# Hybrid encoder layer on one core: the 32 sample tokens taken out of the second half's tiles, computed as one chain for all four heads

## The chip, the cores and the metric

The kernel runs on one core of a Trainium2 chip. The core has a matmul engine (PE, with its weight loads shown apart as PEld), a vector engine (DVE), an activation engine (ACT), a general engine (POOL) and a queue that issues most transfers (SP). Each engine works through its own list of instructions in order and waits on semaphores where it needs what another engine made. The metric is the device time of one execution in microseconds (us); lower is better.

## The reference

One encoder layer is applied to 2048 prompt tokens and, with the same weights, to 32 sample tokens that continue a running stream. What is computed for each of the two groups:

```python
h = rmsnorm(x, g_pre_mix)
z = h @ w_in                                  # 1024 x 2560
u, zq, zf, zi, zg = split(z, [512, 1024, 1536, 2048])
u_ext = concat([pool_hist, u])                # 15 rows of history ahead
y_pool = pool_mix(u_ext, ...)                 # window means over 2/4/8/16 frames minus the frame, per group a linear map
q = silu(zq); fgate = lb + (1 - lb) * sigmoid(zf)
kin = (1 - lb) * sigmoid(-zf); logf = log(fgate)
S1, o = hgrn_run(S0, q, kin, zi, logf)        # gated recurrence, 4 heads x 128, evaluated in chunks
y_hg = rmsnorm(o, g_hg_norm) * silu(zg)
x = x + rmsnorm(concat([y_pool, y_hg]) @ w_out, g_post_mix)
x = x + rmsnorm((silu(h2 @ w_gate) * (h2 @ w_up)) @ w_down, g_post_ffn)   # h2 = rmsnorm(x, g_pre_ffn)
```

The outputs are y for both groups, the last 15 rows of u_ext and the final states S1 of both. The sample tokens start from a given history (15 x 512) and given states (4 x 128 x 128).

## The kernel before, in words

The prompt is worked in two halves of 1024 tokens. Each half goes through the same stages: the value columns of the input product (tile `vps`), for each of four heads the f, q and g columns and then the recurrence (`hgrn`), the four pooling groups, the output product (`project`, tile `ops`), the gate and up products (tiles `gx`, `gy`, `gz`, `gw`). At the end the down product runs over both halves (`dx`, `dy`, `dz`). Large products split each float32 operand into a high and a low part and take three fast 128x512 matmuls for one exact one (`hi`, `lo` in the tile names; `mmb` is the bank of the input product). Small products run on plain float32 operands; each such matmul leaves two records in the profile, a transpose leaves one.

In `hgrn` a head's 1024 tokens are handled in levels: `group` issues 32 small matmuls into the bank `gb`, then `merge` multiplies keys on POOL (`k_t`) and queries on DVE (`qa`) by the gate products of that level, and the next level's `group` needs both. Then come transposes of k (`kps`), state updates (`ups`), outputs (`ops2`, shown as `ops` in the trace), and transposes back (`yps`).

The 32 sample tokens ride with the second half. They are columns 1024 to 1055 of the tiles f, k, q, g and qa (slots of 1088 columns). For each of the 16 column tiles of the second half `sample_tile` multiplies the normalized sample tokens `hsr` with the raw weights in four column groups (`fps`, 8 matmuls), and a step later adds the four parts by a small matmul (`fst`, `fps`). `group` has a 33rd matmul for them, `merge` runs over 1056 columns, and each head ends with a block of its own (L1004 to L1021): one transpose `kps`, three matmuls `ups`, one transpose `yps`, with a state load and a state store. Pooling handles the sample columns in extra small windows (L1051, L1054).

What sets the order: PE's list is written out by the program. Generators (`Task`) hold side work; each `yield` names how much PE time must pass before the next step, and `poll` runs steps that are due after every third large matmul. So a small matmul stands a set number of large matmuls behind what it needs. `join` issues waiting `fps` blocks together with the next `group`. The lists of the other engines are ordered by a scheduler at build time.

Of the kernel before, what the change touches and what calls it, by code (L numbers as in the profile page):

```python
# [29 lines left out]
NT = 21  # L30
# [4 lines left out]
TMAX = HALF + NS  # L35
SLOT = HALF + 64
# [44 lines left out]
def body(tc, ins, outs, cst):  # L81
    nc = tc.nc
    ctx = ExitStack()
    with ctx:
# [69 lines left out]
        roots = DP.tile([1, TMAX], F32, name="roots")  # L154
# [270 lines left out]

        COL_Q, COL_F, COL_I, COL_G = 512, 1024, 1536, 2048
# [5 lines left out]
        def make_half(B):  # L432
            S = Half()
            S.B = B
            S.T = TMAX if B else HALF
# [19 lines left out]
        def later_stats(S):  # L455
# [10 lines left out]
            xs = t2("xsl", [NS, 512]), t2("xsl", [NS, 512])  # L466
            for c in range(2):
                nc.sync.dma_start(out=xs[c], in_=x_s[:, c * 512:c * 512 + 512])
                sumsq(xs[c], NS, st[0:NS, 32 + c:33 + c])
            del xs  # L470
# [7 lines left out]
            nc.gpsimd.tensor_tensor(rt[0:NS, 16:17], st[0:NS, 32:33], st[0:NS, 33:34], ALU.add)  # L478
            nc.gpsimd.tensor_scalar(rt[0:NS, 16:17], rt[0:NS, 16:17], 1.0 / D, EPS, ALU.mult, ALU.add)
            nc.gpsimd.tensor_tensor(rt[0:NS, 17:18], rt[0:NS, 16:17], nhalf[0:NS, 0:1], ALU.pow)  # L480
            roots_out(rt, NCH, roots[0, 0:HALF])
            nc.sync.dma_start(out=roots[0, HALF:TMAX].rearrange("(p i) -> p i", i=1), in_=rt[0:NS, 17:18])

# [19 lines left out]
        def front_norm(S, tg):  # L503
            if tg == 0:
                S.hsr = SP.tile([P, KD, NS], F32, tag="hs", name="hsr", bufs=1)
                S.ysr = SP.tile([P, KD, NS], F32, tag="ysr", name="ysr", bufs=1)
# [3 lines left out]
            if tg == 1:  # L510
                rq = t2("rbs", [P, NS])
                nc.sync.dma_start(out=rq, in_=roots[0:1, HALF:TMAX].broadcast_to([P, NS]))
                nc.sync.dma_start(out=S.hsr, in_=ins["x_sample_channels"].rearrange("(k p) t -> p k t", p=P))
# [3 lines left out]
            if tg == 1:  # L517
                nc.vector.tensor_tensor(S.hsr, S.hsr, rq.unsqueeze(1).broadcast_to([P, KD, NS]), ALU.mult)
                nc.vector.tensor_tensor(S.hsr, S.hsr, g_pre.unsqueeze(2).broadcast_to([P, KD, NS]), ALU.mult)
            yield from scaled_channels(S, tg)  # L520
# [21 lines left out]
        def first_values(S):  # L542
# [41 lines left out]
            nc.sync.dma_start(out=cons[:, 0:C_VEC], in_=cst[:, 0:C_VEC])  # L584
            xg = {}
# [113 lines left out]
            for k in range(0, KD, 2):  # L699
                scaled(k, 0)  # L700

        def values(S, tg):
# [4 lines left out]
            for k in range(0, KD, 2):  # L707
# [12 lines left out]
                if smp:  # L720
                    for kk in range(2):
                        four.add(S.hsr[:, k + kk, :], raw[:, kk * 512:kk * 512 + 512])
            for i in range(4):
                (nc.vector.tensor_copy if i % 2 else nc.scalar.copy)(S.vt[tg * 4 + i], pss[i])
            if smp:
                S.vs = t2("vs")
                nc.gpsimd.memset(S.vs, 0.0)
                sample_sum(S.vs[P - NS:P], sps, 4)

        def sample_tile(S, w, use):  # L730

            if not S.B:
                return None
            raw = w[0]

            def whole():
                task.begun = True
                ps = axbank("fps")
                for k in range(KD):
                    q = k % 4  # L740
                    mm(ps[32 * q:32 * q + 32, 0:P], S.hsr[:, k, :], raw[:, k * P:(k + 1) * P], k < 4, k >= 4, 60.0)
                st = t2("fst", [P, P])
                nc.vector.tensor_copy(st, ps[:, 0:P])
# [8 lines left out]
            return task  # L752
# [8 lines left out]
        def head_products(S, h):  # L761
            H = Half()
            H.f, H.k, H.q, H.g = (ztile(n) for n in ("f_t", "k_t", "q_t", "g_t"))
            def use_f(ps, n0=HALF, n1=TMAX):
# [8 lines left out]
            def use_q(ps, n0=HALF, n1=TMAX):  # L773
# [5 lines left out]
            def use_g(ps, n0=HALF, n1=TMAX):  # L779
# [11 lines left out]
            def tile_of(use):  # L791
                w = take()
                smp = sample_tile(S, w, use)
                blocks_of(w, use, S.blocks)
                return smp

            if h == 0 and not S.B:
                wf, wq = take(), take()
                for blk in S.blocks:
                    blocks_of(wf, use_f, [blk])  # L800
                    blocks_of(wq, use_q, [blk])
            else:
                H.smp = [tile_of(use_f), tile_of(use_q)]
            if h == 0:
                S.attn = [t2(f"attn{i}", [P, 4, P]) for i in range(2)]
                both = [t2(f"cmp{i}") for i in range(2)]
                S.cmp = [tl[:, 0:P].rearrange("p (c x) -> p c x", x=32) for tl in both]
                S.cmps = both[1][:, P:2 * P]
                for tl in S.attn + both:
                    nc.gpsimd.memset(tl, 0.0)  # L810
            task = Task(hgrn(S, H, h), (1800.0 if S.B else 3000.0), after=S.hgrn)
            tile_of(use_g)
# [7 lines left out]
        def hgrn(S, H, h):  # L820
            B, T = S.B, S.T
            for tk in H.smp if B else ():
                tk.finish()
            f_t, k_t, q_t, g_t, vt = H.f, H.k, H.q, H.g, S.vt
            attn, cmp_ = S.attn, S.cmp
            qa = ztile("qa")
            tt = ztile("tt")
            nc.vector.tensor_tensor(qa[:, 0:T], q_t[:, 0:T], f_t[:, 0:T], ALU.mult)
            gb = [axbank("gb") for _ in range(2)]
            blks = [(c, j) for c in range(NCH) for j in range(4)] + [(NCH, 1)] * B  # L830

            def place(c, j, a, b):
                if c < NCH:
                    return gb[c // 4][32 * j:32 * j + 32, c % 4 * 96 + a:c % 4 * 96 + b]
                return gb[1][32:64, 448 + a:448 + b] if b <= 64 else gb[0][32:64, 384 + a:384 + b]

            def group(goff, src, pick, n=16):
                join()
                for c, j in blks:
                    c0 = c * P + 32 * j if c < NCH else HALF  # L840
                    mm(place(c, j, goff, goff + n), k_t[:, c0:c0 + 32], pick(src[:, c0:c0 + 32]), True, True, 36.0)

            def half_of(L):
                return lambda ap: ap.rearrange("p (a two l) -> p a two l", two=2, l=L)[:, :, 1, :]

            toff = 0

            def merge(m, tcur):
                nonlocal toff
                L = 1 << m  # L850
                n = T if m < 5 else HALF
                na = n // (2 * L)
                qv = qa[:, 0:n].rearrange("p (a two l) -> p a two l", two=2, l=L)[:, :, 1, :]
                kv = k_t[:, 0:n].rearrange("p (a two l) -> p a two l", two=2, l=L)[:, :, 0, :]
                tv = tcur[:, 0:2 * na].rearrange("p (a two) -> p a two", two=2)
                nxt = tt[:, toff:toff + na]
                toff += na
# [5 lines left out]
            def masked(dst, view, row0, nch, r):  # L863
                for i in range(NGRP):
                    mk = cons[row0:row0 + r, C_MASK + 16 * i:C_MASK + 16 * i + 16].bitcast(I32).unsqueeze(1).broadcast_to([r, nch, 16])
                    src = view(16 * i, 16 * i + 16) if i in (0, 3, 4, 5) else view(16, 48)
                    if i == 1 or i == 2:
                        src = src.rearrange("p c (b y) -> p c b y", y=4)[:, :, :, 2 * i - 2:2 * i]
                        mk = mk.rearrange("p c (b y) -> p c b y", y=2)
                    if i == 0:  # L870
                        o = dst.rearrange("p c (a two) -> p c a two", two=2)[:, :, :, 0]
                    elif i == 1:
                        o = dst.rearrange("p c (b y two) -> p c b y two", y=2, two=2)[:, :, :, :, 1]
                    elif i == 2:
                        o = dst.rearrange("p c (b two y) -> p c b two y", two=2, y=2)[:, :, :, 1, :]
                    else:
                        L = 1 << (i - 1)
                        o = dst.rearrange("p c (a two l) -> p c a two l", two=2, l=L)[:, :, :, 1, :]
                        mk = mk.rearrange("p c (a l) -> p c a l", l=L)
                        src = src.rearrange("p c (a l) -> p c a l", l=L)  # L880
                    nc.vector.copy_predicated(o, mk, src)

            group(0, q_t, lambda ap: ap.rearrange("p (a two) -> p a two", two=2)[:, :, 0])
            yield 0.0
            tc_ = merge(0, f_t)
            fb = f_t[:, 0:T].rearrange("p (b y) -> p b y", y=4)
            for dst, src in ((fb[:, :, 0:2], q_t[:, 0:T].rearrange("p (b y two) -> p b y two", y=2, two=2)[:, :, :, 1]),
                             (fb[:, :, 2:4], half_of(2)(qa[:, 0:T]))):
                nc.scalar.copy(dst, src)
            yield 5000.0  # L890
            group(16, f_t, lambda ap: ap, 32)
            yield 0.0
            tc_ = merge(1, tc_)
            for m in (2, 3, 4):
                yield (STEP + 900.0 * (h + 1 == NH and m == 4)) if S.B else 1200.0 + 700.0 * (m == 3 and h + 1 < NH)
                group(16 * (m + 1), qa, half_of(1 << m))
                yield 0.0
                tc_ = merge(m, tc_)
# [927 lines left out]
```

## Time and profile before

| | |
|---|---|
| time, 3 runs | 2080.56, 2083.34 and 2084.01 us, median 2083.34 |
| span of the profiled execution | 2079.3 us (its time outside the span is not shown) |
| DMA moved | 319.49 MB, mean 154 GB/s |
| first half: values, columns with recurrence and pooling, output product, gate and up | from 5, 50, 284 and 374 us |
| second half: the same stages | from 797, 843, 1087 and 1184 us |
| down product of both halves | from 1636 us |

The page gives the busy time of each engine as a share of the span, the span in 40 slices, and the costliest groups of instructions. The span runs from the first to the last instruction of the core; the runs' times hold what lies around it too.

### The profile page before, as it was taken

Reading aid. Unit: us, or ns where it says so; the run is one execution under the profiler, and the core shown is the slowest. Engines: PE = TensorE matmul, PEld = TensorE weight load, DVE = VectorE, ACT = ScalarE, POOL = GpSimd, SP = SyncE. Lnnn points to the kernel's source line nnn. Section 1 sums busy time; section 2 is a strip of 40 time slices with the busy share of each in tenths; the row PEclk is TensorE's granted clock in tenths of the full one; section 3 lists DMA queues with packets and bytes.
Section 4 is the critical chain, followed back from the end, with each engine's and each line's share of the span. In section 5 each row is a group of like instructions: output and inputs, shape, how many; then the busy total and the mean of one; then the engine's idle time right before and its main releaser. Section 6 shows DMA issues by size and latency. Waiting matters only on the chain.

```text
span 2079.3 us, 34073 instructions
## 1 busy us (share of the span) xinstructions
PE 2068.0 (99%) x13093; PEld 1686.5 (81%) x13093; DVE 1418.5 (68%) x2288; ACT 834.6 (40%) x1656; POOL 279.7 (13%) x375
## 2 busy tenths in 40 slices
PE   9999999999999999999999999999999999999998
PEld 7788888888888888788888788888888778888876
DVE  5655665787777778465575697776666866566587
ACT  6444445654444445233334563444444521011032
POOL 0232302100000000122231200000000210110134
PEclk9999999999999999999999999999999999999999
DMA  8321144445555558211015614554445796776778
GB/s 288 115 88 42 44 142 162 132 127 167 161 153 152 157 172 260 70 46 36 26 54 177 200 52 137 163 149 139 147 137 173 231 335 203 218 226 200 219 223 220
DMA packets 391777, 319.49 MB, mean 154 GB/s; under 512 B 18216, under 2 KB 320800, under 8 KB 391616
## 3 DMA queue, kind: packets, MB, share of 16 engines
q1 hardware_dynamic: 389168, 309.41, 48.1%
q0 software_dynamic: 2016, 7.34, 1.9%
q8 instruction: 103, 1.69, 0.3%
q10 hardware_dynamic: 432, 0.57, 0.1%
q14 instruction: 58, 0.48, 0.1%
HBM read 216.79 MB, written 100.47 MB: 153 GB/s over the span
## 4 chain that ended last, share of the span: by engine, by line
PE 96%; DVE 2%; DMA 1%; ACT 0%; issue 0%; POOL 0%; DVEq 0%; SPq 0%; ACTq 0%; POOLq 0%
PE gx L202 23%; PE mmb L202 16%; PE gy L202 12%; PE dx L202 10%; PE ops L202 10%; PE gz L202 5%; PE dy L202 5%; PE vps L202 4%; PE dz L202 3%; PE gb L202 1%; PE gw L202 1%; PE gsps L202 1%; PE ups L202 1%; DVE acc L1605 1%; PE tps L345 1%; PE fps L202 1%
## 5 line engine op out<-in xcount | busy, mean ns | idle before, releaser
L202 PE MATMUL gx<-fhi,wf 128*128 128x512 f32 x1376 | 386.9, 391 | 0.0
L202 PEld LDWEIGHTS gx<-fhi,wf 128*128 128x128 f32 x1376 | 256.8, 188 | 54.9 <-issue 2.2
L202 PE MATMUL gx<-flo,wf 128*128 128x512 f32 x688 | 213.1, 390 | 0.0
L202 PE MATMUL gy<-fhi,wf 128*128 128x512 f32 x704 | 201.6, 390 | 0.0
L202 PE MATMUL dx<-dhi,hst 128*128 128x512 f32 x640 | 185.4, 391 | 0.8 <-DVE acc L1605 0.7
L202 PE MATMUL mmb<-hTlo,whi 128*128 128x512 f32 x512 | 175.3, 404 | 0.0
L202 PE MATMUL mmb<-hThi,whi 128*128 128x512 f32 x512 | 165.5, 404 | 0.0
L1605 DVE TENSOR_TENSOR acc<-dx,acc 128x512 f32<-128x512 f32 x168 | 115.1, 690 | 71.6 <-PE dx L202 70.6
L202 PE MATMUL mmb<-hThi,wlo 128*128 128x512 f32 x512 | 158.8, 391 | 0.0
L1325 DVE TENSOR_TENSOR wf<-s,wf 128x512 fp32r<-128x512 f32 x176 | 120.2, 690 | 56.0 <-ACT wf L1320 54.0
L202 PEld LDWEIGHTS gy<-fhi,wf 128*128 128x128 f32 x704 | 131.8, 188 | 28.1 <-DVE c L1427 0.4
L202 PEld LDWEIGHTS gx<-flo,wf 128*128 128x128 f32 x688 | 129.1, 188 | 27.0
L1320 ACT CAST wf<-s 128x512 fp32r<-128x512 f32 x176 | 108.1, 623 | 102.8 <-DVE s L1301 31.5
L202 PEld LDWEIGHTS dx<-dhi,hst 128*128 128x128 f32 x640 | 119.5, 188 | 30.1 <-issue 3.4
L1544 ACT CAST dhi<-t 128x1024 fp32r<-128x1024 f32 x20 | 20.7, 1055 | 249.8 <-DVE dlo L1545 181.6
L1325 DVE TENSOR_TENSOR wf<-wraw,wf 128x512 fp32r<-128x512 f32 x132 | 89.8, 687 | 34.4 <-ACT wf L1320 34.4
L202 PEld LDWEIGHTS mmb<-hTlo,whi 128*128 128x128 f32 x512 | 96.2, 188 | 20.5 <-issue 0.8
L202 PEld LDWEIGHTS mmb<-hThi,wlo 128*128 128x128 f32 x512 | 96.3, 188 | 18.9 <-issue 0.2
L1320 ACT CAST wf<-wraw 128x512 fp32r<-128x512 f32 x132 | 80.8, 622 | 75.8 <-PE gx L202 36.2
L202 PE MATMUL gy<-flo,wf 128*128 128x512 f32 x352 | 108.7, 389 | 0.0
L202 PEld LDWEIGHTS mmb<-hThi,whi 128*128 128x128 f32 x512 | 91.8, 188 | 20.6 <-issue 3.3
L202 PE MATMUL dx<-dlo,hst 128*128 128x512 f32 x320 | 98.6, 389 | 0.0
(326 smaller groups left out, 3974.8 us busy)
## 6 DMA issues: line engine op xcount, KB each, us to landing
hst<-hdFalse SPq DMA_DIRECT2D x140, 256.0 KB, 2.9
hst<-hdTrue SPq DMA_DIRECT2D x140, 256.0 KB, 3.0
wraw<-in_w_gate_dram SPq DMA_DIRECT2D x50, 512.0 KB, 4.0
wraw<-in_w_up_dram SPq DMA_DIRECT2D x50, 512.0 KB, 3.9
hdFalse<-hhi SPq DMA_DIRECT2D x77, 256.0 KB, 2.3
hdFalse<-hlo SPq DMA_DIRECT2D x77, 256.0 KB, 2.2
hdTrue<-hhi SPq DMA_DIRECT2D x77, 256.0 KB, 2.2
hdTrue<-hlo SPq DMA_DIRECT2D x77, 256.0 KB, 2.5
```

What stands on the lines that cost most here:

```text
L202: nc.tensor.matmul(out, l, r, start=start, stop=stop, skip_group_check=more)
L345: nc.tensor.transpose(ps[:, c:c + P], xn[:, (2 * kp + kk) * P:(2 * kp + kk + 1) * P], ident)
L1320: nc.scalar.copy(wf[:, 0], getattr(M, src) if isinstance(src, str) else src)
L1325: nc.vector.tensor_tensor(wf[:, 1], getattr(M, src) if isinstance(src, str) else src, wf[:, 0].bitcast(F32), ALU.subtract)
L1544: nc.scalar.copy(hi, src)
L1605: nc.vector.tensor_tensor(dst, ps, dst, ALU.add)
```

## The change

The sample tokens leave the tiles of the second half. Their raw channels are loaded at the start (`sample_loads`) and multiplied by g_pre on POOL; the tokens are loaded once more, four times over in the partitions, for their root mean squares (`sample_stats`). `sample_tile` now runs in the first half, when the same weight tiles pass, and scales by the root when it copies `fps` out; the results of all heads and groups lie in one tile `z` (128 channels x f, q, g, u x 4 heads x 32 tokens). After the values of the second half one task, `sample_mix`, does for all four heads at once what was done per head: gates, five levels on a 128-column tile (4 matmuls a level, bank `xgb`), one transpose `kps`, one output of five matmuls with a block matrix (`ops2`), one 512-wide state update (`ups`), one transpose back. The pooling windows of the prompt lose the 15 history columns ahead and run the first 31 columns in small tiles of their own (`eh`). The slots of the large pool shrink from 1088 to 1024 columns, and the pool of 512-column tiles has 25 buffers where it had 21.

```diff
-NT = 21
+NT = 25
...
-TMAX = HALF + NS
-SLOT = HALF + 64
+SLOT = HALF
...
+        def sample_loads():
+            Smp.hsr = SP.tile([P, KD, NS], F32, tag="hs", name="hsr", bufs=1)
+            Smp.z = SP.tile([P, 4, P], F32, tag="xz", name="xz", bufs=1)
...
+            nc.sync.dma_start(out=Smp.hsr, in_=ins["x_sample_channels"].rearrange("(k p) t -> p k t", p=P))
+            Smp.x = [t2("xs4") for _ in range(2)]
+            for q in range(8):
+                r, c = q // 2 * 32, q % 2
+                nc.sync.dma_start(out=Smp.x[c][r:r + 32], in_=x_s[:, c * 512:c * 512 + 512])
+        def sample_stats():
+            nc.gpsimd.tensor_tensor(Smp.hsr, Smp.hsr, g_pre.unsqueeze(2).broadcast_to([P, KD, NS]), ALU.mult)
+            st = small("xst", [P, 4], bufs=1)
+            for c in range(2):
+                sumsq(Smp.x[c], P, st[:, c:c + 1])
...
+            Smp.rs = rstd_of(st, P, True)
...
-        def sample_tile(S, w, use):
-            if not S.B:
-                return None
+        def sample_tile(S, w, kind, h):
+            if S.B:
+                return
...
-                nc.vector.tensor_copy(st, ps[:, 0:P])
+                nc.vector.tensor_scalar(st, ps[:, 0:P], Smp.rs, None, ALU.mult)
                 yield 5000.0
                 zs = ps[:, P:P + NS]
                 mm(zs, st, cons[:, C_I4:C_I4 + NS], True, True, 215.0)
-                use(zs)
+                nc.vector.tensor_copy(Smp.z[:, kind, h * NS:(h + 1) * NS], zs)
...
-            task = Task(whole(), 6500.0)
+            task = Task(whole(), 6500.0 if h or kind > 1 else 14000.0)
...
+        def sample_mix():
+            z, v = Smp.z, nc.vector
+            s0 = t2("xs0", [P, NH, P])
+            nc.sync.dma_start(out=s0, in_=ins["state_hgrn"][0, 0].rearrange("h k v -> k h v"))
...
+            nc.scalar.activation(sg[:, 0:3], z[:, 0:3], AF.Sigmoid)
+            nc.scalar.activation(sg[:, 3], z[:, 0], AF.Sigmoid, scale=-1.0)
+            f, k, q, qa = (w[:, i] for i in range(4))
+            v.tensor_tensor(heads_of(f), heads_of(sg[:, 0]), by_head(oml), ALU.mult)
+            v.tensor_tensor(heads_of(f), heads_of(f), by_head(lb), ALU.add)
+            v.tensor_tensor(heads_of(k), heads_of(sg[:, 3]), by_head(oml), ALU.mult)
+            v.tensor_tensor(q, z[:, 1], sg[:, 1], ALU.mult)
...
+            yield 2500.0
...
+            gb = axbank("xgb")
+            L = Levels(P, k, qa, at[:, 1], lambda c, j, a, b: gb[32 * j:32 * j + 32, a:b], [(0, j) for j in range(4)])
+            L.group(0, q, EVEN)
+            yield 0.0
+            tc_ = L.merge(0, f)
+            L.pairs_of(f, q)
+            yield 3000.0
+            L.group(16, f, lambda ap: ap, 32)
+            yield 0.0
+            tc_ = L.merge(1, tc_)
+            for m in (2, 3, 4):
+                yield 2000.0
+                L.group(16 * (m + 1), qa, half_of(1 << m))
+                yield 0.0
+                tc_ = L.merge(m, tc_)
...
+            nc.tensor.transpose(kps[:, 0:P], k, ident)
...
+            mm(ops[:, 0:P], at[:, 0], rows, True, False, 218.0)
+            for h in range(NH):
+                mm(ops[:, 0:P], qb[:, h], s0[:, h], False, h == NH - 1, 218.0)
+            on = out_stage(ops, 1, P)
+            ups = axbank("ups")
+            mm(ups, kd, vb, True, True, 858.0)
...
+            yield 4000.0
+            yps = back(on, 1, P)
...
             if B:
                 nc.sync.dma_start(out=outs[3][0, 0, h], in_=s_cur)
-                s0 = small("S0", [P, P], bufs=2)
-                nc.sync.dma_start(out=s0, in_=ins["state_hgrn"][0, 0, h])
-                kps = axbank("kps")
-                nc.tensor.transpose(kps[:, 0:P], k_t[:, TMAX - P:TMAX], ident)
...
-                mm(ups[:, 0:P], kd, S.vs[:, hs], True, True, 218.0)
-                mm(ups[:, P:2 * P], qa[:, TMAX - P:TMAX], s0, True, False, 218.0)
-                mm(ups[:, P:2 * P], S.cmps, S.vs[:, hs], False, True, 218.0)
...
-                yps = back(on, 1, P)
```

**PE, second half.** In the time of the next head's large matmuls PE had each head's sample block in three pieces: the transpose `kps` of L1006, twelve large matmuls on the three matmuls `ups`, and later the transpose `yps`. The middle piece of the first head (names as in the text above; numbers are buffers), before:

```order
L202 MATMUL mmb<-hTlo_7409,whi 128x512
L202 MATMUL mmb<-hThi_7406,wlo 128x512
L202 MATMUL mmb<-hThi_7408,wlo 128x512
L202 MATMUL ups<-vs,kds 128x128
L202 MATMUL ups<-S_8776,qa 128x128
L202 MATMUL ups<-vs,cmp_8159 128x128
L202 MATMUL mmb<-hThi_7410,whi 128x512
L202 MATMUL mmb<-hThi_7412,whi 128x512
```

The three pieces are gone for each of the four heads. In their place PE has, right behind the values of the second half, the chain for all heads. Its first level, 15 large matmuls behind the last value matmuls of the sample tokens (`vsps`), after:

```order
L201 MATMUL mmb<-hTlo_7650,whi 128x512
L201 MATMUL mmb<-hTlo_7652,whi 128x512
L201 MATMUL mmb<-hThi_7649,wlo 128x512
L201 MATMUL mmb<-hThi_7651,wlo 128x512
L201 MATMUL mmb<-hThi_7653,whi 128x512
L201 MATMUL mmb<-hThi_7655,whi 128x512
L201 MATMUL mmb<-hTlo_7654,whi 128x512
L201 MATMUL xgb<-xw 32x16 x4
L201 MATMUL mmb<-hTlo_7656,whi 128x512
L201 MATMUL mmb<-hThi_7653,wlo 128x512
```

and its end, which leads into the first level of the first head:

```order
L201 MATMUL mmb<-hThi_7649,whi 128x512
L201 MATMUL mmb<-hThi_7651,whi 128x512
L201 MATMUL mmb<-hTlo_7650,whi 128x512
L201 MATMUL ops_8496<-xat 128x128
L201 MATMUL ops_8496<-xs_8223,xqb 128x128 x4
L201 MATMUL ups<-xvb,xes 128x512
L201 MATMUL gb<-q_t,k_t 32x16 x32
L201 MATMUL mmb<-hTlo_7652,whi 128x512
```

What moved: the twelve pieces of four heads became five levels, one pair of transposes, one block of six matmuls and one transpose, all of them by the time of the first head's own first levels.

**DVE, start of the second half.** Behind the last copies of the values DVE added the four parts of the sample values (`vs`) and went on with the first head's gates. Before:

```order
L724 COPY va<-vps 128x512
L724 COPY vb<-vps 128x512
L406 TENSOR_TENSOR vs<-vsps,vs 32x512 x3
L768 TENSOR_SCALAR f_t<-sg,lbt 128x512
L771 TENSOR_SCALAR k_t<-sg,lbt 128x512
L743 COPY fst<-fps 128x128
L1250 TENSOR_TENSOR hlo<-hs,hhi 128x512
```

After, where `xw` holds the sample tokens' f, k, q and qa, and `xsg` the sigmoids:

```order
L729 COPY va<-vps 128x512
L729 COPY vb<-vps 128x512
L925 COPY xes<-xz 128x4x32
L405 TENSOR_TENSOR vs<-vsps,vs 32x512 x3
L919 TENSOR_TENSOR xw<-xsg,lbt 128x128
L921 TENSOR_TENSOR xw<-xsg,lbt 128x128
L920 TENSOR_TENSOR xw<-xw,lbt 128x128
L922 TENSOR_TENSOR xw<-xz,xsg 128x128
L923 SCALAR_TENSOR_TENSOR xsg<-xz,cons,xsg 128x128
L924 TENSOR_TENSOR xw<-xw 128x128
L932 TENSOR_SCALAR xat<-vs,xst 32x128 x4
```

What moved: DVE copies `xes` and makes f, k and q of all heads here, behind the three additions to `vs`.

**DVE, first half, between two heads.** After the transposes back of a head (`yr`, `ylo`) DVE makes qa of the next and runs the first merge. Before:

```order
L996 TENSOR_TENSOR yr<-yps,g_t 128x512 x2
L818 TENSOR_TENSOR ylo<-yr,yhi 128x512
L828 TENSOR_TENSOR qa<-q_t,f_t 128x1024
L818 TENSOR_TENSOR ylo<-yr,yhi 128x512
L859 TENSOR_TENSOR qa<-qa,f_t 128x512
L860 TENSOR_TENSOR tt<-f_t 128x512
L783 SCALAR_TENSOR_TENSOR g_t<-mmb,cons,sg 128x512
```

After:

```order
L1093 TENSOR_TENSOR yr<-yps,g_t 128x512 x2
L822 TENSOR_TENSOR ylo<-yr,yhi 128x512
L1001 TENSOR_TENSOR qa<-q_t,f_t 128x1024
L822 TENSOR_TENSOR ylo<-yr,yhi 128x512
L748 TENSOR_SCALAR fst<-fps,xst 128x128
L849 TENSOR_TENSOR qa<-qa,f_t 128x512
L850 TENSOR_TENSOR tt<-f_t 128x512
```

What moved: the copy `fst` of a sample block that PE now issues in the first half stands ahead of the merge.

More of the change, by code (lines that the diff above doesn't have):

```diff
@@ L861, in merge @@
                 return nxt
[L863 to L881, printed above, removed]
@@ L883, in hgrn, with pairs_of @@
-            group(0, q_t, lambda ap: ap.rearrange("p (a two) -> p a two", two=2)[:, :, 0])
-            yield 0.0
[L885 to L889, printed above, removed]
+            def pairs_of(self, f_t, q_t):
+                n = self.n
+                fb = f_t[:, 0:n].rearrange("p (b y) -> p b y", y=4)
+                for dst, src in ((fb[:, :, 0:2], q_t[:, 0:n].rearrange("p (b y two) -> p b y two", y=2, two=2)[:, :, :, 1]),
+                                 (fb[:, :, 2:4], half_of(2)(self.qa[:, 0:n]))):
+                    nc.scalar.copy(dst, src)
@@ new lines, in pool_tail, with hgrn @@
+        def pool_tail(out, tail):
+            n = 4 * HIST
+            ps = axbank("nps")
+            nc.tensor.transpose(ps[0:n, 0:P], tail.rearrange("p g t -> p (g t)"), ident)
+            tick(107)
+            npl = small("npl", [n, P], bufs=1)
+            nc.vector.tensor_copy(npl, ps[0:n, 0:P])
+            for g in range(4):
+                nc.sync.dma_start(out=out[0, 0, :, g * P:(g + 1) * P], in_=npl[g * HIST:(g + 1) * HIST])
+        def hgrn(S, H, h):
+            B = S.B
+            f_t, k_t, q_t, g_t, vt = H.f, H.k, H.q, H.g, S.vt
+            attn, cmp_ = S.attn, S.cmp
+            qa = ztile("qa")
+            nc.vector.tensor_tensor(qa, q_t, f_t, ALU.mult)
+            gb = [axbank("gb") for _ in range(2)]
+            L = Levels(HALF, k_t, qa, ztile("tt"), lambda c, j, a, b: gb[c // 4][32 * j:32 * j + 32, c % 4 * 96 + a:c % 4 * 96 + b],
+                       [(c, j) for c in range(NCH) for j in range(4)])
+            L.group(0, q_t, EVEN)
+            yield 0.0
+            tc_ = L.merge(0, f_t)
+            L.pairs_of(f_t, q_t)
@@ L1069, in pool_window @@
             put_y(S, g, slice(0, HALF), d)
-            if S.B:
+            if S.B and g == 0:
                 yield 0.0
-                yield from window(es, NS, [small(n, [P, 48], bufs=1) for n in ("es1", "es2")], S.ysr[:, g, :], False)
-                if g == 0:
-                    ps = axbank("nps")
-                    nc.tensor.transpose(ps[0:8 * HIST, 0:P], S.tail.rearrange("p s g t -> p (s g t)"), ident)
-                    tick(107)
-                    npl = small("S0", [8 * HIST, P], bufs=2)
-                    nc.vector.tensor_copy(npl, ps[0:8 * HIST, 0:P])
-                    for i in range(8):
-                        out = outs[4 if i // 4 else 2]
-                        nc.sync.dma_start(out=out[0, 0, :, i % 4 * P:(i % 4 + 1) * P], in_=npl[i * HIST:(i + 1) * HIST])
+                pool_tail(outs[2], S.tail)
         def project(S, tg):
             smp = S.B and tg == 1
+            if smp:
+                Smp.mix.finish()
             yms = [ztile("ym", [P, D]) for _ in range(4)]
```

292 lines of the change are left out of this document (154 added, 138 removed).

## The prediction

> **What bounds the kernel now.** I read the page's summary first, then the wait list of PE, then the busy time by stage. Page:
>
> ```profile
> span 2079.3 us, 34073 instructions
> ...
> PE 2068.0 (99%) x13093; PEld 1686.5 (81%) x13093; DVE 1418.5 (68%) x2288; ACT 834.6 (40%) x1656; POOL 279.7 (13%) x375
> ...
> PE 96%; DVE 2%; DMA 1%; ACT 0%; issue 0%; POOL 0%; DVEq 0%; SPq 0%; ACTq 0%; POOLq 0%
> ```
>
> PE is busy 99% of the span, and 96% of the chain that ended last is PE. Matmul ends are modelled, so busy alone proves little; the wait list must agree. All of it that has PE as the waiter:
>
> ```profile
> PE idle L202 <- POOL ones L145: 1.1, 1, 1.1
> PE vps L202 <- ACT xg L590: 0.9, 1, 0.9
> PE dx L202 <- DVE acc L1605: 0.7, 2, 0.4
> PE gb L202 <- ACT f_t L889: 0.3, 2, 0.2
> PE dx L202 <- DMA hst<-hdTrue: 0.2, 1, 0.2
> ```
>
> The columns are total us, times and longest. In 2079 us PE waits 3.2 us for anybody, and 2.0 of these are at the start. By stages (first number in us, then PE busy):
>
> ```profile
> 60.00:270.00 210.00, 209.60 (x2401) 1.00 0.23 72
> 840.00:1085.00 245.00, 245.00 (x2851) 1.00 0.15 43
> ```
>
> The second half's mixing stage, from which the sample tokens are taken, has no PE wait at all, and the first half's, into which they go, 0.4 us. So DVE, ACT and POOL work that leaves the second half saves nothing: PE hides it already. Only what changes in PE's own list, or a new PE wait, can move the time.
>
> **PE's list, from start times.** One large matmul costs the distance of starts:
>
> ```profile
> 914.96 0.62 PE L202 MATMUL mmb<-hThi,wlo 128*128 128x512 f32 x2
> 915.43 0.27 PE L1006 MATMUL kps<-cons,k_t 128*128 128x128 f32 x1
> 915.45 0.71 PE L202 MATMUL mmb<-hThi,whi 128*128 128x512 f32 x2
> 916.00 0.62 PE L202 MATMUL mmb<-hTlo,whi 128*128 128x512 f32 x2
> 916.46 0.63 PE L202 MATMUL mmb<-hThi,wlo 128*128 128x512 f32 x2
> ...
> 917.83 0.62 PE L202 MATMUL mmb<-hThi,wlo 128*128 128x512 f32 x2
> 918.29 0.38 PE L202 MATMUL ups<-vs,kds 128*128 128x128 f32 x2
> 918.51 0.39 PE L202 MATMUL ups<-S,qa 128*128 128x128 f32 x2
> 918.74 0.39 PE L202 MATMUL ups<-vs,cmp 128*128 128x128 f32 x2
> 918.88 0.71 PE L202 MATMUL mmb<-hThi,whi 128*128 128x512 f32 x2
> 919.43 0.63 PE L202 MATMUL mmb<-hTlo,whi 128*128 128x512 f32 x2
> ```
>
> From 916.00 to 916.46 two take 0.46, so 0.23 each. From 914.96 to 916.00 four large ones (0.92) and one transpose take 1.04: a lone transpose costs 0.12. From 917.83 to 919.43 four large ones and the three `ups` take 1.60: the block costs 0.68, with 0.22 to 0.23 from one float32 matmul to the next.
>
> ```profile
> 89.48 0.62 PE L202 MATMUL mmb<-hThi,wlo 128*128 128x512 f32 x2
> 89.93 1.02 PE L202 MATMUL wmp<-wmr,wpt 128*128 128x512 f32 x2
> 90.39 1.02 PE L202 MATMUL mmb<-hThi,whi 128*128 128x512 f32 x2
> 91.25 0.40 PE L202 MATMUL mmb<-hTlo,whi 128*128 128x512 f32 x1
> 91.58 0.74 PE L202 MATMUL gb<-qa,k_t 128*32 128x16 f32 x64
> 92.24 0.50 PE L202 MATMUL mmb<-hTlo,whi 128*128 128x512 f32 x1
> 92.58 0.63 PE L202 MATMUL mmb<-hThi,wlo 128*128 128x512 f32 x2
> ```
>
> From 89.48 to 91.25 four large ones and one 512-wide float32 matmul take 1.77: 0.85 for it. From 91.25 to 92.58 two large ones and a level of 32 small matmuls (64 records) take 1.33: 0.87 for the level. Of this the small ones take at most 0.66/32 = 0.02 each; the rest is the price of entering and leaving such a block. A level of 4 costs 0.87 less 28 x 0.02 = 0.31; with 0.017, what the 0.66 gives if 0.1 of it is the exit, 0.39. I take 0.37.
>
> *Removed:* per head two lone transposes (0.24) and the three `ups` (0.68), times four 3.7; the 33rd matmuls, five per head, 20 x 0.017 = 0.3. Together **4.0 us**.
>
> *Added:* five `xgb` levels of 4, 5 x 0.37 = 1.85; `kps` and the sample's own `nps` in one block, 0.23; five `ops2` matmuls 5 x 0.22 = 1.1 and the 512-wide `ups` 0.85 to 0.95; one transpose back 0.12. Together **4.2 us**.
>
> *Moved:* the 16 `fps` blocks with their 16 small sums, the same matmuls on the same weights, again joined to a `gb` level where one is due. By the order of both programs PE goes from large to small matmuls 195 times before and 197 times after, and issues 11 fewer matmuls. So PE's list comes out **+0.2 us**, with bounds of -0.2 (0.31 a level, 0.85) and +0.4 (0.39, 0.95). Eleven fewer matmuls buy nothing, because blocks of transposes and 128-wide matmuls, which cost almost nothing to enter, are replaced by blocks of 32-column matmuls, which cost 0.3.
>
> [...]
>
> **The new waits.** The first `xgb` needs the sample tokens' q. Rows of before at that place:
>
> ```profile
> 841.76 1.06 PE L202 MATMUL vsps<-wrow,hsr 128*32 128x512 f32 x8
> 842.76 0.73 PE L202 MATMUL mmb<-hThi,whi 128*128 128x512 f32 x2
> ...
> 842.94 0.57 ACT L404 COPY vs<-vsps 32x512 f32<-32x512 f32 x1 [1.84 <-PE vsps L202]
> 848.57 1.28 ACT L767 ACT_TABLE_LOAD   x1 [5.05 <-PE mmb L202]
> ...
> 843.55 2.14 DVE L406 TENSOR_TENSOR vs<-vsps,vs 32x512 f32<-32x512 f32 x3 [0.98 <-ACT vs L404]
> ...
> L860 DVE TENSOR_TENSOR tt<-tt 128x128 f32<-128x128 f32 x4 | 1.1, 287 | 0.1
> L767 ACT ACTIVATE sg<-fps 128x32 f32<-128x32 f32 x4 | 0.8, 201 | 8.4 <-PE fps L202 8.4
> ```
>
> On before's clock: 15 large matmuls behind 842.76, and 0.1 for leaving the small block, put the first `xgb` at 842.76 + 15 x 0.23 + 0.1 = 846.3. On ACT the copy ends at 843.5, the table load now comes at once and ends at 844.8, and the two sigmoids (0.2 for 32 columns here; for 384, 0.45, my value) end at 845.45. On DVE the additions end at 845.7, and f, k, f and q stand behind them in its list: four operations at 0.2 to 0.29, so q is there at 846.5 to 846.9. PE waits **0.5 us** (bounds 0 and 1.0). Behind it in PE's list stand the first head's large matmuls; nobody else waits for them. Later levels have 15 or 16 large matmuls (3.5 us) each for a 64-column merge on POOL and DVE and two ACT copies: I cost them at nothing, covered by about 1 us. The transpose back has some 2.9 us behind `ops2` for a square, two POOL operations, and a product; covered, narrowly.
>
> In the first half `fst` stands ahead of the merge whose copies PE already waits 0.2 for, twice (`f_t` above). It adds 0.3 on DVE there, but a joined `fps` block gives PE 0.2 of other work: **+0.2** for the four heads, between -0.3 and +1.5. The two squares at the start of the first half (0.8 each by other squares) fall into idle ACT time. Narrower slots and four more 512-column buffers I put at 0: start distances are 0.227 to 0.23 in all stages, whichever pool the operands come from, and no wait names a full pool. The bounds are -1 (the 0.9 of `dx` waits goes) and +1. On SP's queue `hsr` is followed by eight pieces of `xs`, where four transfers stood:
>
> ```profile
> 24.88 0.38 SPq L513 DMA_DIRECT2D hsr<-x_sample_channels  x1
> ...
> 30.64 0.43 SPq L253 DMA_DIRECT2D wraw<-in_w_in_dram  x1
> ```
>
> Nine at some 0.4 from 24.9 end at 28.5, before the next weight load is issued at 30.6, so they cost nothing; if they pushed it back by some us, PE would wait for `wraw` there.
>
> **Sum:** 0.2 + 0.5 + 0.2 = +0.9 on the span of 2079.3, which makes 2080.2. The runs lie 1.3 to 4.7 above that span and their median, 2083.34, lies 4.0 above; what surrounds the span is not touched. So **2084.2 us**.
>
> **Rivals.**
>
> *A. The sample chain is late at every step (slower).* DVE works in order, and a merge on POOL and one on DVE of the same level collide:
>
> ```profile
> 100.56 1.54 DVE L859 TENSOR_TENSOR qa<-qa,tt 128x512 f32<-128x512 f32 x1
> ...
> 100.50 1.06 POOL L858 TENSOR_TENSOR k_t<-k_t,tt 128x512 f32<-128x512 f32 x1 [2.71 <-issue]
> ```
>
> The DVE merge, 0.68 alone, took 1.54 beside POOL's. [...] If one step of the sample chain, from a level's end to the next level's operands, takes over 3.5 us, each of the nine points where PE meets the chain stalls; at 0.6 each that is 5.4, so 2089. Against it: 64 columns are an eighth of these, and POOL is 13% busy.
>
> *B. The first half pays.* All 16 `fst` and `z` copies now sit in a stage that already had waits. At 0.5 at three places a head, 2 to 3 us for the heads that have no slack: 2086.
>
> *C. PE's list shrinks after all (faster).* If entering and leaving small blocks were free, the count alone would decide: 12 less 5 matmuls of 0.22, five fewer transposes of 0.11, one of 0.85 more, which is -1.2. If in addition the large matmuls of the second half's mixing stage (half of the 1536 with `mmb`) went from 0.23 to the 0.227 of other stages, 768 x 0.003 = -2.3 more: 2080.
>
> *D. The change doesn't do what it says.* If the removed second-half work had been hiding something, PE's waits there would not be 0; nothing more to gain or lose. It gives 2083.3 and is inside the forecast.
>
> **How the numbers follow.** Forecast with D 0.69 (2082 to 2086), B 0.12, A 0.09, C 0.10. The runs before lie up to 2.8 below and 0.7 above their median; with the bounds of the sum (its lower ends together 2.4 below the values taken, its upper ones 3.0 above) the range is 2080.0 to 2087.5 and holds the forecast, B and most of C. 0.2%, about what a measurement of this kernel can tell from no change, is 4.2 us. Only A passes it upward (0.09, and 0.01 for a tail of B); C at 2080 does not reach it, its tail does (0.07 with what I don't see), and 0.83 stays between.
>
> **What would show it.** Right: the profile after has PE 99% busy, a wait of `xgb` on DVE of about 0.5, no other new PE wait above 0.3, and a span within 2 us of 2079.3. Wrong in the list: the distances around `xgb` levels of 4 are not near 0.37. Wrong in the waits: `fps`, `gb` or `yps` in PE's wait list with a total over 2 us. Wrong altogether: start distances of large matmuls that differ from 0.227 to 0.23.

## The result and the profile after

The changed kernel takes **2090.0 us** (median of 5 runs, 2087.44 to 2090.49), the kernel before 2081.29 (5 runs, 2080.56 to 2084.01): a ratio of 1.0034, 95% interval 1.0022 to 1.0046. By the ratio it is slower by some 7 us, three tenths of a per cent; the two medians lie 8.7 apart. It is above the range that was forecast. The profiled execution took 2090.05 us with a span of 2088.3, which is 9.0 above the span before; the stages below are read from these two executions.

The page's summary of the changed kernel:

```profile
span 2088.3 us, 33924 instructions
...
PE 2072.6 (99%) x13076; PEld 1686.3 (81%) x13076; DVE 1422.8 (68%) x2288; ACT 829.1 (40%) x1635; POOL 298.7 (14%) x402
```

PE is busy 99% of the span again, and its busy time has grown by only 4.6 us of the 9.0. The share hides the change; the wait list of PE does not (total us, times, longest; left out are the start, the down stage and one `gb` of 0.3):

```profile
PE kps L1056 <- POOL k_t L848: 2.4, 1, 2.4
...
PE gy L201 <- DVE c L1488: 1.0, 1, 1.0
PE yps L898 <- DVE on L891: 0.7, 2, 0.5
...
PE mmb L201 <- ACT hThi L646: 0.5, 2, 0.4
```

One line leads: PE waits 2.4 us for the `k_t` that POOL's last merge makes, ahead of the transposes `kps` in the last head of the first half. Busy time by stage tells where it lies. Before (stretch and its length, PE busy and its instructions, granted clock, DMA share, GB/s):

```profile
49.70:283.50 233.80, 233.40 (x2506) 1.00 0.25 78
842.80:1086.50 243.70, 243.70 (x2845) 1.00 0.15 44
1086.50:1184.00 97.50, 97.50 (x467) 1.00 0.49 162
```

After, the same stages, cut at the same matmuls:

```profile
49.60:303.90 254.30, 250.37 (x2792) 0.99 0.25 77
863.60:1096.00 232.40, 232.09 (x2556) 1.00 0.18 53
1096.00:1191.60 95.60, 95.60 (x451) 1.00 0.47 156
```

The second half's mixing gives back 11.3 us and its projection 1.9, as work that was moved should; the first half's mixing takes 20.5 more. Its idle time went from 0.4 to 3.9 us, and its granted clock is 0.99. The rest of the span grew by 1.7, most of it one wait of 1.0 for `gy`.

Behind the long wait the clock falls (the same columns, changed kernel):

```profile
262.00:265.00 3.00, 0.73 (x4) 1.00 0.00 0
265.00:267.00 2.00, 1.87 (x25) 0.87 0.00 0
267.00:269.00 2.00, 2.00 (x7) 0.50 0.77 219
269.00:270.50 1.50, 1.50 (x11) 0.70 0.15 57
```

Length times what the clock lacks is 0.26 + 1.0 + 0.45 = 1.7 us lost behind a wait of 2.4. A wait list doesn't show this part: PE counts as busy.

**Why `k_t` came late.** The engine timelines (start, duration) show the last head of the first half. Behind `lv`, the last level's matmuls, POOL copies blocks of the tile `cmp`, which DVE fills with the masked entries of `gb`, into the tile `attn`, and then makes the last `k_t`. Before: POOL, the first wide add of the pool window on DVE, and PE's transpose:

```profile
242.22 4.91 POOL L929 COPY attn<-cmp 32x128 f32<-32x128 f32 x8 [0.23 <-DVE cmp L881]
247.22 1.91 POOL L858 TENSOR_TENSOR k_t<-k_t,tt 128x512 f32<-128x512 f32 x1
...
243.77 1.24 DVE L1051 TENSOR_TENSOR sa<-e_t 128x1038 f32<-128x1038 f32 x1 [0.89 <-ACT e_t L1036]
...
249.24 1.04 PE L959 MATMUL kps<-cons,k_t 128*128 128x128 f32 x8
```

POOL's merge ended at 249.13, and PE began the transposes at 249.24. PE did not wait, but the slack was 0.1 us. After, POOL and DVE:

```profile
255.55 2.25 POOL L1045 COPY attn<-cmp 32x128 f32<-32x128 f32 x4 [0.23 <-DVE cmp L878]
257.86 0.20 POOL L1120 COPY eh<-e_t 128x16 f32<-128x16 f32 x1
...
258.49 4.53 POOL L1045 COPY attn<-cmp 32x128 f32<-32x128 f32 x4 [0.29 <-PE lv L201]
263.10 1.97 POOL L848 TENSOR_TENSOR k_t<-k_t,tt 128x512 f32<-128x512 f32 x1
...
256.42 1.23 DVE L1126 TENSOR_TENSOR sa<-e_t 128x1023 f32<-128x1023 f32 x1 [0.48 <-ACT e_t L1110]
258.09 0.19 DVE L1127 TENSOR_TENSOR eh<-eh 128x30 f32<-128x30 f32 x1 [0.45 <-POOL eh L1120]
258.20 0.23 DVE L878 COPY_PREDICATED cmp<-cons,gb 128x64 f32<-128x64 int32 x1
258.33 1.22 DVE L1126 TENSOR_TENSOR sb<-sa 128x1021 f32<-128x1021 f32 x1
```

Eight copies took 4.9 us before and 6.8 after, with 0.7 between the two groups. Wide adds (1.2 us) ran beside the copies before as well, but the first began 1.55 us behind the first copy; now it begins 0.87 behind it. At the 0.3 us that run 7 shows for a copy without an add beside it, three of the eight were stretched before and five are now; this is an estimate from the sums. Two things are new in these rows. The first add now stands even ahead of the last `cmp` copy, on which the second four `attn` copies depend; and a copy for the window's new head (`eh`) stands in POOL's queue, for which DVE waits. The experiments set these apart.

**Why the scaled channels came late.** SP's queue before and after, with DVE's first scaling of each:

```profile
35.22 0.35 SPq L669 DMA_DIRECT2D rb<-roots_a  x1
...
39.38 1.42 DVE L641 SCALAR_TENSOR_TENSOR xc<-xc,cons,rb 128x512 f32<-128x512 f32 x2 [0.86 <-DMA rb<-roots_a]
```

```profile
25.51 8.41 SPq L485 DMA_DIRECT2D xs<-in_x_sample_dram  x8
...
38.40 0.35 SPq L673 DMA_DIRECT2D rb<-roots_a  x1
...
43.05 1.42 DVE L645 SCALAR_TENSOR_TENSOR xc<-xc,cons,rb 128x512 f32<-128x512 f32 x2 [2.93 <-DMA rb<-roots_a]
```

The eight loads of the sample rows take 8.4 us of SP's queue, 1.05 each. The load of the roots is issued 3.2 us later, and scaling starts 3.7 later. PE meets that 24 us further on:

```profile
62.95 0.62 PE L201 MATMUL mmb<-hThi,wlo 128*128 128x512 f32 x2
63.92 0.49 PE L201 MATMUL mmb<-hThi,whi 128*128 128x512 f32 x1 [0.35 <-ACT hThi L646]
64.59 0.50 PE L201 MATMUL mmb<-hThi,whi 128*128 128x512 f32 x1 [0.17 <-ACT hThi L646]
64.99 1.10 PE L201 MATMUL mmb<-hTlo,whi 128*128 128x512 f32 x2
65.93 0.62 PE L201 MATMUL mmb<-hThi,wlo 128*128 128x512 f32 x2
```

Six large matmuls fill the 2.98 us from 62.95 to 65.93; at 0.227 each they need 1.36, so 1.6 us went there, of which the wait list names 0.5. In the trace before, no such gap stands at this place.

### The profile page after: what moved, and what is told of

It is laid out like the page before. It is cut to its first block, busy times and chain, and to the rows that moved or that the text cites. A ratio compares the mean times of both kernels' runs of the same rounds, so it can differ in the third digit from the quotient of the medians.

```text
span 2088.3 us, 33924 instructions
## 1 busy us (share of the span) xinstructions
PE 2072.6 (99%) x13076; PEld 1686.3 (81%) x13076; DVE 1422.8 (68%) x2288; ACT 829.1 (40%) x1635; POOL 298.7 (14%) x402
## 4 chain that ended last, share of the span: by engine, by line
PE 92%; DVE 4%; DMA 2%; POOL 1%; issue 1%; ACT 1%; SPq 0%; DVEq 0%; POOLq 0%; ACTq 0%
PE gx L201 22%; PE mmb L201 16%; PE gy L201 11%; PE dx L201 10%; PE ops L201 10%; PE dy L201 5%; PE gz L201 5%; PE dz L201 3%; PE vps L201 2%; PE gb L201 1%; PE gw L201 1%; DVE acc L1666 1%; PE gsps L201 1%; PE ups L201 1%; PE tps L344 1%
## 5 line engine op out<-in xcount | busy, mean ns | idle before, releaser
L1381 ACT CAST wf<-s 128x512 fp32r<-128x512 f32 x176 | 107.9, 621 | 104.1 <-DVE s L1362 31.5
```

The source lines that it names most:

```text
L1381: nc.scalar.copy(wf[:, 0], getattr(M, src) if isinstance(src, str) else src)
```

## The experiments

All ratios are against the kernel before on the same chip, whose median lay between 2081.85 and 2083.03.

**Run 1. Loads of the sample rows in two issues.**

```diff
-for q in range(8):
-    r, c = q // 2 * 32, q % 2
-    nc.sync.dma_start(out=Smp.x[c][r:r + 32], in_=x_s[:, c * 512:c * 512 + 512])
+for c in range(2):
+    nc.sync.dma_start(out=Smp.x[c], in_=x_s[:, c * 512:c * 512 + 512].unsqueeze(0).broadcast_to([4, NS, 512]))
```

> The changed kernel with its eight loads of the sample rows made in two transfers, each of which writes all four copies. Theory (SP's queue): eight issues of 1.05 us each push the next weight load and the load of the roots back by 3.3 us, and with them the scaled channels, for which PE then waits between 63 and 68 us (1.7 us in all). With two issues the roots are issued near 35.5 us, that wait is below 0.3, and the time falls by 1.5 to 2, to about 2088. Rival (the new squares and the table load on ACT make the channels late): the waits at 63 to 68 us stay and the time stays at 2090.

A miss: 2091.24, ratio 1.0036 (1.0023 to 1.0049), where about 2088 was expected. The two issues took 3.3 us, but what stood behind them waited as well, and the roots were loaded at 40.0, later still. The waits for `hThi` stayed. Fewer issues of the same bytes on the same queue freed nothing; the test did not take the loads off the path, so it left the cause open.

**Run 2. The sample rows from POOL's queue.**

```diff
-nc.sync.dma_start(out=Smp.x[c][r:r + 32], in_=x_s[:, c * 512:c * 512 + 512])
+nc.gpsimd.dma_start(out=Smp.x[c][r:r + 32], in_=x_s[:, c * 512:c * 512 + 512])
```

> The changed kernel with its eight loads of the sample rows issued from POOL's queue, which is empty there, instead of SP's. Theory (SP's queue): the next weight load is issued near 26 to 31 us and the load of the roots near 35, the scaled channels start near 40 instead of 43, the waits of PE between 63 and 68 us go, and the time falls by 1.5 to 2, to 2088. Rival (the 0.5 MB of rows fill the DMA engines, from whichever queue): the roots' load still lands late, the waits stay, and so does 2090.

2087.87, ratio 1.0027 (1.0017 to 1.0036). SP's load of the roots and DVE's first scaling in its profile:

```profile
36.55 0.35 SPq L673 DMA_DIRECT2D rb<-roots_a  x1
...
40.79 1.42 DVE L645 SCALAR_TENSOR_TENSOR xc<-xc,cons,rb 128x512 f32<-128x512 f32 x2
```

The roots come 1.9 us earlier and scaling 2.3. The wait for `hThi` is gone from PE's list, so the queue was the cause, and not the bytes, which are the same. The `kps` wait is still there with its 2.40 us; in this one profiled execution (2084.61) the clock behind it stayed at 1.00, and nine other runs lie between 2086.3 and 2090.1.

**Run 3. The window's head copies on DVE.**

```diff
-nc.gpsimd.tensor_copy(eh[0][:, 0:HIST], hist[:, g, 0:HIST])
-nc.gpsimd.tensor_copy(eh[0][:, HIST:n], e_t[:, 0:16])
+nc.vector.tensor_copy(eh[0][:, 0:HIST], hist[:, g, 0:HIST])
+nc.vector.tensor_copy(eh[0][:, HIST:n], e_t[:, 0:16])
```

> The changed kernel with the two copies that make up the pool window's head (15 columns of history, 16 of this half) on DVE instead of POOL. Theory 1 (the new copy in POOL's queue): in the last head of the first half the copy stands between two attn groups, DVE's list waits for it, and the k merge comes 2.4 us late; without it the kps wait is below 1 us and the time falls by 2 to 4, to 2086 to 2088. Theory 2 (the two engines hold each other up whatever the copy does: 1.2 us adds of the window on DVE stretch POOL's attn copies from 0.29 to 1.27): the kps wait stays at 1.5 or more and the time at 2088.5 to 2091.

2089.18, ratio 1.0030 (1.0018 to 1.0041). The `kps` wait is still 2.1 us, and POOL's second group of copies as long as ever:

```profile
258.92 4.53 POOL L1045 COPY attn<-cmp 32x128 f32<-32x128 f32 x4
```

The copy in POOL's queue is worth a few tenths. Theory 1 falls as the main cause, and theory 2 forecast both the wait and the time.

**Run 4. The last head's `attn` copies on ACT.**

```diff
-nc.gpsimd.tensor_copy(attn[sb][...], cmp_[sb][...])
+cp = nc.scalar.copy if not B and h + 1 == NH else nc.gpsimd.tensor_copy
+cp(attn[sb][...], cmp_[sb][...])
```

> The changed kernel with the eight attn copies of the first half's last head on ACT instead of POOL, so that the k merge is next in POOL's queue. Both theories on POOL: no kps wait at 262 us, and no stretch of half clock behind it, so 2.4 us of wait and about 1.6 of slow clock go: 2086. Rival (k is late because of DVE's part, the products of decays or the merge of q): the wait stays above 1.5 and the time at 2089 to 2091.

2085.63, ratio 1.0014 (1.0004 to 1.0023). No `kps` wait is left in the list, and PEclk is 1.00 in all stretches from 255 to 267 us. By the two ratios, 1.0034 and 1.0014, that wait and its slow clock are worth about 4 us, more than half of the loss.

**Run 5. Two waits added to the kernel before.** Products of `k_t` with 1 on POOL ahead of the last head's `kps`: two as shown, and one in a second kernel.

```diff
 t7 = merge(6, tc_)
+if not B and h + 1 == NH:
+    for _ in range(2):
+        nc.gpsimd.tensor_tensor(k_t[:, 0:512], k_t[:, 0:512], ones[:, 0:1].broadcast_to([P, 512]), ALU.mult)
```

> The kernel before with two products of k with 1 added on POOL ahead of the last head's kps in the first half, of the size of a merge step: PE should wait there 2 to 4 us. Theory (a wait of some 2.4 us also lowers the granted clock for a stretch): PEclk falls to about 0.5 for 3 to 4 us behind the wait, and the span grows by the wait and 1.5 to 2 us more (to 2083 to 2085). Rival (the slow stretch seen in the changed kernel came from something else in it): the clock stays at 1.0 and the span grows by the wait alone.

> The kernel before with one added product on POOL in place of two: PE should wait there 1.2 to 2. If every wait lowered the clock, the span would grow by the wait and 1.6 more; if a wait must be longer than some 2.3 us (one of 2.1 us left the clock at 1.0, one of 2.4 did not), PEclk stays at 1.0 and the time grows by the wait alone, to 2084 to 2085.

With two products PE waits 3.7 us and the time is 2088.12 against 2083.03, 5.1 more. The windows behind the wait:

```profile
253.00:255.00 2.00, 1.64 (x9) 0.56 0.00 0
255.00:257.00 2.00, 2.00 (x10) 0.58 0.20 28
257.00:259.00 2.00, 2.00 (x17) 1.00 0.64 235
```

By the same reckoning as above 1.7 us are lost to the clock. With one product PE waits 1.8, the clock stays at 1.00, and the time is 2084.48 against 2082.31, 2.2 more. So a kernel that has nothing of the change shows the same slow stretch behind a long wait and none behind a short one, each in one profiled execution.

**Run 6. The new window alone, and the old window put back.** The first takes the kernel before and makes its first half's windows as the change does; the second takes the changed kernel and makes its windows as before.

```diff
-SLOT = HALF + 64
+SLOT = HALF + 48
...
-nc.gpsimd.tensor_copy(hist[:, g, 0:HIST], e_t[:, HALF:HALF + HIST])
+nc.gpsimd.tensor_copy(eh[0][:, 0:HIST], hist[:, g, 0:HIST])
+nc.gpsimd.tensor_copy(eh[0][:, HIST:n], e_t[:, 0:16])
...
+    nc.vector.tensor_tensor(nxt[:, q:HALF], cur[:, q:HALF], cur[:, q - lev:HALF - lev], ALU.add)
+    nc.vector.tensor_tensor(nh[:, q:n], ch[:, q:n], ch[:, q - lev:n - lev], ALU.add)
```

> The kernel before with the change's new form of the pool window in the first half alone (1024 columns, the first 16 made apart from copies on POOL); slots of 1072 columns for 1088, and nothing of the sample tokens moved. Theory 1 (the new window itself makes k late): PE waits 1.5 to 2.5 for the last head's kps, and the time is 2085 to 2087. Theory 2 (it is the window's place beside the head's last steps that matters, and this comes from the sample blocks put into the first half): in the instruction lists all twelve cmp copies still stand ahead of the first add, the kps wait stays below 0.4 and the time within 1 of before, 2083.

```diff
-NT = 25
+NT = 20
...
-e_t = ztile("e_t")
+e_t = ztile("e_t", [P, HALF + 64])
+nc.vector.tensor_copy(e_t[:, 0:HIST], hist[:, g, 0:HIST])
...
-nc.vector.tensor_tensor(nxt[:, a:HALF], cur[:, a:HALF], cur[:, a - lev:HALF - lev], ALU.add)
-nc.vector.tensor_tensor(nh[:, a:n], ch[:, a:n], ch[:, a - lev:n - lev], ALU.add)
+nc.vector.tensor_tensor(nxt[:, p:n], cur[:, p:n], cur[:, p - lev:n - lev], ALU.add)
```

> The changed kernel with the pool window of before in both halves (15 columns of history ahead of the half, no copies of the head on POOL); its three tiles of 1088 columns, which widens all slots to that, and 20 buffers of 512 columns for 25. Theory 1 (the copies of the new window in POOL's queue): the kps wait falls below 0.7. Theory 2 (place): the first add still stands ahead of the last cmp copy in DVE's list, POOL's attn copies still run beside adds, and the kps wait stays between 1.2 and 2.2. The time is not the measure here, as fewer buffers may cost elsewhere; by theory 1 it would be near 2086, by theory 2 near 2089.

The new window alone leaves no `kps` wait in PE's list; its time, 2113.91, is another matter (run 8). The old window in the changed kernel leaves a `kps` wait of 1.7 us and 2089.1, ratio 1.0033 (1.0021 to 1.0045). Its time is no measure: its profile has another wait of 2.1 us for a `gb` at 197 us, for which the trace names no releaser. So the new form of the window neither makes the wait nor, taken away, ends it. That leaves the window's place, which run 7 tests. In DVE's list the first add stands ahead of the last `cmp` copy both in the changed kernel and in this one, and behind it in both kernels without the sample blocks.

**Run 7. The first window begun later.**

```diff
-S.pools[g] = S.pool = Task(pool_window(S, g, e_t), 1500.0, after=S.pool)
+S.pools[g] = S.pool = Task(pool_window(S, g, e_t), 1500.0 + 7500.0 * (not S.B and S.pool is None), after=S.pool)
```

> The changed kernel with the first pool window of the first half begun 7.5 us later by the planner's clock, which puts its wide adds behind all twelve cmp copies and behind the last merge of q in DVE's list; POOL keeps its attn copies, the new copies of the head and the k merge. Theory (POOL's copies are stretched by the adds beside them): the copies take 0.3 each again, the kps wait is below 0.3, no slow clock follows, and the time falls by 3 to 4.5, to 2085.5 to 2087. Rival (POOL's list itself is too long there): the wait stays above 1.5, and so does 2089 to 2090.

2083.95 against 2081.85, ratio 1.0009 (0.9999 to 1.0019), better than the 2085.5 to 2087 expected; the wait of 0.5 for the last head's `yps` in the first half went too. POOL, with everything of the change still in its list, and DVE's first add:

```profile
255.35 1.28 POOL L1045 COPY attn<-cmp 32x128 f32<-32x128 f32 x4 [0.23 <-DVE cmp L878]
256.69 0.20 POOL L1120 COPY eh<-e_t 128x16 f32<-128x16 f32 x1
...
256.98 1.28 POOL L1045 COPY attn<-cmp 32x128 f32<-32x128 f32 x4
...
259.12 1.88 POOL L848 TENSOR_TENSOR k_t<-k_t,tt 128x512 f32<-128x512 f32 x1
...
258.88 1.22 DVE L1126 TENSOR_TENSOR sa<-e_t 128x1023 f32<-128x1023 f32 x1
```

The first add now starts when the last `attn` copy has ended (258.26). Four copies take 1.28 us where they took 2.25 and 4.53, the `kps` wait is gone, and so is the clock's stretch. This is the same work with the adds moved out from beside the copies, so the collision is shown to be the cause of the `kps` wait, and POOL's own load is not.

**Run 8. Slots of 1072 columns, in the kernel before.**

```diff
-SLOT = HALF + 64
+SLOT = HALF + 48
```

> The kernel before with slots of 1072 columns for 1088 and nothing else, since the kernel with the new window alone ran 30 us longer with every large matmul at 231 to 232 ns for 227. If the width of the slots does that, it shows here too: 2105 to 2112 and 231 ns. If it was the window, 2083 and 227 ns.

One run, 2113.8 against 2082.31. PE's timeline in the first gate and up stage:

```profile
500.24 0.62 PE L202 MATMUL gx<-fhi,wf 128*128 128x512 f32 x2
500.70 0.62 PE L202 MATMUL gx<-flo,wf 128*128 128x512 f32 x2
501.17 1.09 PE L202 MATMUL gx<-fhi,wf 128*128 128x512 f32 x4
502.10 0.62 PE L202 MATMUL gx<-flo,wf 128*128 128x512 f32 x2
```

The eight large matmuls from 500.24 to 502.10 stand 0.232 apart. At the same place it is 0.227 in the kernel before (slots of 1088) and in the changed kernel (1024), and 0.232 in the window-alone kernel of run 6 (ten from 500.12 to 502.44), which has slots of 1072 as well and took 2113.91 us. By an estimate, 0.005 more for each of the stage's 1881 PE instructions is 9 of the 31.5 us between 2113.8 and 2082.31, and 31.5 over the 8232 large matmuls in the trace before is 0.004 each: other stages must have been slower too. The time of the window-alone kernel is put down to the slots, and its wait list alone was used above.

**Run 9. Both mends, and three steps moved.** First the edits of runs 2 and 4 together, then also:

```diff
-yield 800.0 if S.B and sb == 0 else 4500.0
+yield 800.0 if S.B and sb == 0 else 4500.0 + 900.0 * (h + 1 == NH and not S.B)
...
-yield 4000.0
+yield 5200.0
 yps = back(on, 1, P)
...
-yield (STEP + 900.0 * (h + 1 == NH and m == 4)) if S.B else 1200.0 + 700.0 * (m == 3 and h + 1 < NH)
+yield (STEP + 900.0 * (h + 1 == NH and m == 4)) if S.B else 1200.0 + 700.0 * (m == 3)
```

> The two edits together: the sample rows from POOL's queue, and the attn copies of the first half's last head on ACT. If the two causes are separate their gains add up: 4.4 of the one (measured) and 1.7 of the other, so 2084. If they hang together, not under 2085.

> Both edits that helped (sample rows from POOL's queue, the last head's attn copies on ACT), and more large matmuls ahead of three steps for which PE still waits: 0.9 us ahead of the last head's transpose back in the first half, 1.2 ahead of the sample's, and 0.7 ahead of the last head's fourth level. The waits are 0.6, 0.4 and 0.4 now: if they go and nothing takes their place, the time is 2082.4, 0.2 to 0.7 below or level with the kernel before. If the steps only move and meet the next one late, it stays at 2083.8 or above.

Together 2083.77, ratio 1.0003 (0.9994 to 1.0013); with the three steps 2083.24, ratio 1.0001 (0.9992 to 1.0010). The gains of the two edits add up, as expected; the three steps brought 0.5 us where 1.4 was hoped for, less than the spread of the runs. What is left of the changed kernel's waits in PE's list of the last one:

```profile
PE yps L898 <- DVE on L891: 0.2, 1, 0.2
PE gy L201 <- DVE c L1489: 0.2, 1, 0.2
```

The `yps` wait left is that of the second half's last head, not of the sample tokens, so the second of the three steps was moved to no purpose. Without its waits the change is level with the kernel before, and not faster. No kernel here beats it.

## Why the prediction was wrong

- **What bounds the kernel** (PE, by its list and its waits): right. Of the 9.0 us of the span, 4.1 are the `kps` wait and its slow clock, 1.6 the loss at 63 us, 1.0 the wait for `gy`, 0.7 the waits for `yps` and 0.5 PE's longer list; for the last 1 us no single row was found.
- **PE's list, +0.2 us:** right within what can be read, if a little low. In the last kernel of run 9 the first half's mixing stage takes 247.1 us, the second's 232.6 and the two projections 91.0 and 95.6, which is 0.5 more than before for the four stages that the change touches (the bounds were -0.2 and +0.4). The rows agree too; a level of four in the changed kernel:

```profile
871.54 0.39 PE L201 MATMUL mmb<-hTlo,whi 128*128 128x512 f32 x1
871.86 0.27 PE L201 MATMUL xgb<-xw 128*32 128x32 f32 x8
872.06 0.50 PE L201 MATMUL mmb<-hTlo,whi 128*128 128x512 f32 x1
872.40 0.63 PE L201 MATMUL mmb<-hThi,wlo 128*128 128x512 f32 x2
```

  From 871.54 to 872.40 are 0.86, less two large ones 0.40 (predicted 0.37). Going into the block costs 0.09 of it (871.54 to 871.86 is 0.32 for one large matmul against 0.23).
- **The sample chain, 0.5 us for the first `xgb`, and rival A:** PE's list names no wait for any of the chain's steps. Into the first `xgb` PE takes 0.45 us for one large matmul (866.92 to 867.37) where the level above takes 0.32, so 0.1 went there, not 0.5. The 0.45 us for a sigmoid of 384 columns was the author's estimate; ACT took 0.53 for it (at 865.66, L916). The chain in the second half, to which most of the working went, was the harmless part.
- **"Nine at some 0.4 from 24.9 end at 28.5 ... so they cost nothing": failed.** The size was taken from one row of another transfer. The trace before has rows of 1 us each for transfers issued in a run on this queue:

```profile
13.94 4.09 SPq L575 DMA_DIRECT2D xt<-in_x_prompt_dram  x4
```

  In the changed kernel the eight took 1.05 each. The text's own proviso (PE would wait if the weight load were pushed back) came true in another way: PE waited not for `wraw` but for the channels that the roots scale, 1.6 us.
- **The first half, +0.2 between -0.3 and +1.5: failed, and most of the loss is here.** The step asked who stands beside the joined blocks and took "no wait" before for cover. It never looked how much slack the head's chain had: 0.1 us at `kps`. It also left the pool window's rewriting without a price and without a look at its neighbours in DVE's and POOL's lists. What the runs showed in its place is a longer collision of DVE's adds with POOL's copies, worth 2.4 us of wait, and a slow clock behind it, worth 1.7, for which no term stood at all. Rows of such a collision stood in the prediction itself, under rival A, but it was looked for in the sample chain alone.
- **Rival B** (the first half pays) had the right place and sign at 2086, but spread over three places a head; it was one head, once, with the clock on top.
- **From the span to the time, +4.0:** too much. Each of the five runs of the changed kernel lies 1.7 to 1.8 above its own span. The other 2.3 were the difference between the profiled execution before and the median of three others, which became 2081.29 with two more. With 1.75 the same sum gives 2082.0, so the steps on the span missed by 8 us and not by 5.8. The sum's own bounds and the spread of the runs give 2079.0 to 2087.9, a little wider than the range stated; the result lies above both.
- **Narrower slots at 0:** right for 1024 columns against 1088 (0.227 us in both); that 1072 would come out 31 us longer (run 8, one run) was not foreseen.

Two things stay open. Which of the moved pieces brought the window's adds forward beside the copies was not separated. What can be counted in PE's rows is how far: the large matmuls that the first add needs (through `e_t`) now end nine large matmuls ahead of `lv`, and ended six ahead before. That is one step of `poll`, 0.7 us, and only the kernels with the sample blocks in the first half show it. And the wait for `gy` in the second gate and up stage is between 0 and 1.2 us over these profiles, in variants of both kernels; its cause was not settled.

## What to carry to other kernels

No wait before does not mean slack: for each step that a change comes near, read how long before its use the operand was ready, and let that number bound what may be added. Price a transfer on a queue by rows where several are issued in a run, and follow what is queued behind it to the first wait. And when work leaves one stage for another, look at what now runs side by side on DVE and POOL there, not only at how busy they are: POOL was busy 14% of the span and still late.

## What was new of the hardware

- **Behind some long waits of PE the granted clock fell.** It was 0.87, 0.50 and 0.70 in the windows from 265 to 270.5 us behind a wait of 2.4 us (changed kernel), 0.70, 0.50 and 0.95 from 266 to 272 behind one of 2.4 us (run 1), and 0.56 and 0.58 from 253 to 257 behind one of 3.7 us (run 5): 1.7 us lost each time. Behind waits of 1.7 us (run 6), 1.8 us (run 5) and 2.1 us (run 3) it stayed at 1.00, and behind the same 2.40 us in run 2 too, so in these profiles the length alone does not decide.
- **A POOL copy of 0.3 us became one of 1.1** beside DVE adds of 1.2 us (four in 1.28 us in run 7, and in 4.53 in the changed kernel).
- **With slots of 1072 columns large matmuls stood 0.232 us apart, and 0.227 with 1024 and 1088**, read at one place of the first gate and up stage (run 8, and the window-alone kernel of run 6). Why was not tried.
